# The second MLP product by Strassen's seven products of halves, with activations and sums kept in DRAM

## The chip, the cores and the metric

One core of a Trainium2 chip runs the whole kernel in one launch. The metric is the device time of one execution, in microseconds (us). Engines are named as in the profile: PE (TensorE, matrix products; PEld is its weight load), DVE (VectorE), ACT (ScalarE), POOL (GpSimd, here an issuer of DMAs), SP (SyncE, the other issuer of DMAs).

## The reference

One layer over 1024 latent tokens and 256 context tokens, width 1024. A mixer with two head groups (RG-LRU and S5), an output projection, a first layer norm, and then the part that the change touches:

```
def sq_relu_mlp(x, w1, b1, w2, b2):
    return jnp.square(jax.nn.relu(x @ w1 + b1)) @ w2 + b2
...
        x = layer_norm(DEEPNORM_ALPHA * x + g1 * m_lat, ln1_g[l], ln1_b[l])
        f_lat = sq_relu_mlp(modulate(x, sh2, sc2), mlp_w1[l], mlp_b1[l], mlp_w2[l], mlp_b2[l])
        x = layer_norm(DEEPNORM_ALPHA * x + g2 * f_lat, ln2_g[l], ln2_b[l])
```

Here `x` is 1024 x 1024, `w1` 1024 x 4096, `w2` 4096 x 1024, all float32.

## The kernel before

Everything is computed transposed: features lie on the 128 partitions, tokens on the free axis. Float32 products are made of three products of rounded parts: each operand is split into a high part (a cast to the format fp32r) and a low part (the value less its high part), and PE multiplies high by high, high by low and low by high, all into one PSUM sum. `split` makes such a pair for weights: ACT casts (`wh`), DVE subtracts (`wl`). `weights` loads 512 KB on SP's queue into `wr` (three buffers) and calls `split`.

The MLP starts when the first layer norm's results are there as `x2`: eight tiles, one for 128 features, with high and low parts of 1024 tokens. Tokens go in two halves j = 0, 1 of 512. The norm of half 0 is finished before the MLP; that of half 1 (its tiles are `yb`, `lt`, `lq`) runs on DVE and ACT under the first products of the MLP, as the generator `steps`.

The first product has 32 tiles of 128 hidden features. For one tile and one half, `prod` (L666 on, matmul at L675) makes 24 matmuls of 512 columns (8 tiles of `x2` by 3 parts). ACT then takes the relu (`r`) and the square (`hh`, the high part), DVE squares again in float32 and subtracts (`hl`, the low part).

The second product (`mlp2`, matmul at L1062) runs in nine blocks, `BLK = (3, 3, 3, 3, 4, 4, 4, 4, 4)`, right after the hidden tiles of its block. For each of 8 tiles of output features and each half it sums the block's tiles in PSUM, and DVE adds that to `acc` in SBUF. The last block goes in 256 columns and ends in the second layer norm (`centre`, `scale`) and the output DMAs. So hidden tiles never leave SBUF, and the hidden tiles and the weights of a block are all that is needed at once.

A scheduler sets the order of instructions on every engine from the order of the code and from when it takes things to be ready; each engine then runs its list strictly in order, so an instruction that waits holds everything behind it on its engine. A tile with `bufs=n` has n buffers; the writer of the next one waits for the last user of the oldest, a DMA that reads it among them. DMAs are issued in order on SP's queue (`ld`), on ACT's (`st_`), and on POOL's (`G.dma_start`), and `program` gives the descriptors of POOL's queue a small room in SBUF: `dynamic_dma_scratch_size=1024`, bytes a partition.

Of the kernel before, what the change touches and what calls it, by code (L numbers as in the profile page):

```python
# [41 lines left out]
def build(nc, tc, a, out):  # L42
# [967 lines left out]
    acc = {}  # L1010

    relu = [None]

    def mlp1(ids):
        ws = [weights(a["w1"][i]) for i in ids]
        hs = [[mp.tile([P, NL], F32R, tag=t, name=t, bufs=5) for t in ("hh", "hl")] for i in ids]
        yield hs
        for j in range(2):
            js = HS[j]
            for i, w, (hh, hl) in zip(ids, ws, hs):  # L1020
                ps = psm_.tile([P, 512], F32, tag="m1", name="ps_m1", bufs=3)
                prod(ps, w, x2, js)
                r = mp.tile([P, 512], F32, tag="r", name="r", bufs=2)
                S.activation(r, ps, AF.Relu, bias=col("b1", i))  # L1024
                relu[0] = S.activation(hh[:, js], r, AF.Square)  # L1025
# [4 lines left out]
    def weights2(i, last=False):  # L1030
        p, n = (mp, 3) if i % 4 < 3 else (mp2[0], 1)
        raw = wp.tile([P, 1024], F32, tag="wr", name="wr", bufs=3)
        ld(raw, a["w2"][i])
        hi = p.tile([P, D], F32R, tag="w2h", name="w2h", bufs=n)
        lo = p.tile([P, D], F32R, tag="w2l", name="w2l", bufs=n)
        if last:

            wm = mp2[0].tile([P, row(1)], F32, tag="wm", name="wm", bufs=4)[:, 0:1]
            stt(raw, raw, 1.0, g2r[0], MUL, MUL, accum_out=wm)
            ts(wm, wm, -1.0 / D, MUL)  # L1040
            S.activation(hi, raw, AF.Identity, bias=wm)
            stt(lo, raw, wm, f(hi), ADD, SUB)
        else:
            S.copy(hi, raw)  # L1044
            tt(lo, raw, f(hi), SUB)
# [4 lines left out]
    NB = len(BLK)  # L1050

    def mlp2(b, o, n, ws, hs, bk):
        last = b == NB - 1
        js = slice(o, o + n)
        for m in range(8):
            ps = psm_.tile([P, n], F32, tag="m2", name="ps_m2", bufs=3)
            c = 0
            for i in range(bk):
                hh, hl = hs[i]
                wh, wl = ws[i]  # L1060
                for x, w in ((hh, wh), (hl, wh), (hh, wl)):
                    PE.matmul(ps, w[:, m * P:(m + 1) * P], x[:, js], start=(c == 0), stop=(c == 3 * bk - 1))  # L1062
                    c += 1
            if b == 0:
                if m % 2 == 0:
                    acc[m // 2, o // 512] = (mp2[0] if o else mp).tile([P, 2, 512], F32, name=f"acc{m // 2}_{o // 512}")
            ac = acc[m // 2, o // 512][:, m % 2, o % 512:o % 512 + n]
            if b == 0:
                (S.copy if m % 2 else V.tensor_copy)(ac, ps)
            elif not last:  # L1070
                tt(ac, ps, ac, ADD)
            else:
                tt(ac, ps, ac, ADD)
            if b == NB - 2:
                nt = mp.tile([P, 512], F32, tag="r", name="nin", bufs=2)
                ld(nt, nscr[m, o // 512])
                ts(nt, nt, cr[:, m:m + 1], MUL, cd[:, m:m + 1], ADD)
                stt(ac, ac, g2c[:, m:m + 1], nt, MUL, ADD)
                if m == 0:
                    now = centre(n)  # L1080
                    next(now)
                now.send(ac)
            if last:
                if m == 0:
                    now = scale(mp2[0], n, "f", done2(js), o == NL - n)
                    next(now)
                now.send(ac)
            next(steps2[0], None)
            next(steps2[0], None)
        for _ in steps2[0]:  # L1090
            pass
        if b >= NB - 2:
            steps2[0] = now
        if last and o == NL - n:
            for _ in now:
                pass
# [12 lines left out]
    mp2 = []  # L1109
    i0 = 0  # L1110
    for b, bk in enumerate(BLK):
        ids = list(range(i0, i0 + bk))
        i0 += bk
        if b == 0:

            one = mlp1(ids)
            hs = next(one)
        else:
            hs = []
            for i in ids:  # L1120
                one = mlp1([i])
                hs += next(one)
                for _ in one:
                    pass
        if b:
            ws = [weights2(i, b == NB - 1) for i in ids]
        for o in range(0, NL, 256 if b == NB - 1 else 512):
            if b == 0:
                next(one)
                if o == 0:  # L1130
                    ws = [weights2(i) for i in ids]
            mlp2(b, o, 256 if b == NB - 1 else 512, ws, hs, bk)
            if b == 0 and o == 0:
                fence[0] = relu[0]
                for _ in steps:
                    pass
                dst_.close()
                mp2.append(pool("mp2", stack=mlp))
                g2r.append(mp2[0].tile([P, D], F32, name="g2r"))
                d = dr.tile([8, P], F32, name="g2d")  # L1140
                ld(d.rearrange("m p -> p m"), g2c)
                ld(g2r[0], d.rearrange("m p -> (m p)").partition_broadcast(P))
# [90 lines left out]
```

## Time and profile before

| what | us |
|---|---|
| median of 3 runs | 1647.38 (1646.48 to 1650.17) |
| the profiled execution | 1642.92 |
| its span, first to last instruction | 1641.1 |
| PE's first product of the MLP starts at | 908.68 |
| first half-1 product of the MLP starts at | 947.22 |

Times in the rows are counted from the span's start. A matmul of 512 columns is shown with 0.39 us, but the next one starts 0.23 us after it: matmuls are pipelined, so their cost is read from the distance of their starts, or from the chain of waits, where a run of xN of them has one length. "Busy" of PE is therefore high wherever matmuls follow one another.

### The profile page before, as it was taken

The numbers are of one execution on the slowest core, as the hardware profiler recorded it, in microseconds if no ns is written. First come the engines' busy times: TensorE is split into PE (matmuls) and PEld (weight loads), VectorE is DVE, ScalarE is ACT, GpSimd is POOL, SyncE is SP. The second block draws the span as 40 slices with busy tenths as digits, with TensorE's granted clock in tenths as the row PEclk, the third lists the DMA queues.
The fourth block names the chain that finished last, engine by engine and source line by source line (L and its number), as shares of the span: only waits on it lengthen the run. The fifth ranks groups of instructions, "written<-read, shape, count | busy, mean of one in ns | idle before, by whom it ended". The sixth has DMA issues, their size and how long they took to land.

```text
span 1641.1 us, 20069 instructions
## 1 busy us (share of the span) xinstructions
PE 1552.9 (95%) x7508; PEld 1268.1 (77%) x7508; DVE 1109.4 (68%) x2371; ACT 710.2 (43%) x978; POOL 8.7 (1%) x37
## 2 busy tenths in 40 slices
PE   7899998999879999799999899999999999999997
PEld 2687777777758787697788678888888888888887
DVE  7999999998939899329878844333432334247856
ACT  5576666666792426743335642113130303031225
POOL 0000000000000000000000000000000000000000
PEclk9999999999999999899999999999999999999999
DMA  7533323333745836855686421111110202022202
GB/s 270 203 119 112 106 109 117 120 115 108 271 139 176 239 129 165 220 155 200 197 281 192 169 92 63 39 39 64 52 52 20 70 13 90 13 77 84 71 1 103
DMA packets 92721, 199.27 MB, mean 121 GB/s; under 512 B 12496, under 2 KB 43728, under 8 KB 91472
## 3 DMA queue, kind: packets, MB, share of 16 engines
q1 hardware_dynamic: 77424, 176.10, 33.4%
q10 hardware_dynamic: 14048, 17.70, 3.0%
q0 software_dynamic: 1152, 4.19, 1.1%
q8 instruction: 59, 0.97, 0.2%
q14 instruction: 38, 0.31, 0.1%
HBM read 153.98 MB, written 43.98 MB: 121 GB/s over the span
## 4 chain that ended last, share of the span: by engine, by line
PE 58%; DVE 24%; ACT 7%; DMA 6%; issue 5%; SPq 0%; ACTq 0%; DVEq 0%
PE ps_m L675 22%; PE ps_m L1062 21%; PE ps_g L435 3%; PE ps_mm L380 3%; DVE sT L47 2%; DMA mo<-in_ada_t 2%; DVE wl L47 2%; DVE H L47 2%; DVE xc L56 2%; DVE sU L47 2%; DVE ii L47 2%; ACT H L603 1%; PE ps_gl L694 1%; DVE rr L56 1%; DVE ii L455 1%
## 5 line engine op out<-in xcount | busy, mean ns | idle before, releaser
L675 PE MATMUL ps_m<-x,wh 128*128 128x512 f32 x1024 | 323.2, 396 | 5.5 <-DVE yb L47 5.5
L675 PEld LDWEIGHTS ps_m<-x,wh 128*128 128x128 f32 x1024 | 192.6, 188 | 54.1 <-issue 6.1
L1062 PE MATMUL ps_m<-hh,w2h 128*128 128x512 f32 (+1 forms) x576 | 211.2, 367 | 0.0
L1062 PE MATMUL ps_m<-hl,w2h 128*128 128x512 f32 (+1 forms) x576 | 210.9, 366 | 0.0
L1062 PE MATMUL ps_m<-hh,w2l 128*128 128x512 f32 (+1 forms) x576 | 210.9, 366 | 0.0
L675 PE MATMUL ps_m<-x,wl 128*128 128x512 f32 x512 | 203.0, 397 | 0.0
L47 DVE TENSOR_TENSOR acc<-ps_m,acc 128x512 f32<-128x512 f32 (+1 forms) x144 | 90.7, 630 | 141.6 <-PE ps_m L1062 140.8
L98 ACT CAST wh<-wr 128x1024 fp32r<-128x1024 f32 x88 | 92.1, 1050 | 208.3 <-PE ps_m L675 102.7
L47 DVE TENSOR_TENSOR wl<-wr,wh 128x1024 fp32r<-128x1024 f32 x88 | 107.2, 1220 | 107.0 <-ACT wh L98 106.8
L380 PE MATMUL ps_mm<-x0h,wh 128*128 128x512 f32 x352 | 139.8, 397 | 1.0 <-ACT wh L98 1.0
L380 PE MATMUL ps_mm<-x0h,wl 128*128 128x512 f32 x352 | 139.5, 397 | 0.9 <-DVE wl L47 0.9
L380 PE MATMUL ps_mm<-x0l,wh 128*128 128x512 f32 x352 | 139.5, 396 | 0.0
L1044 ACT CAST w2h<-wr 128x1024 fp32r<-128x1024 f32 x28 | 28.7, 1049 | 236.1 <-PE ps_m L1062 206.5
L1062 PEld LDWEIGHTS ps_m<-hh,w2h 128*128 128x128 f32 x576 | 108.6, 189 | 18.3 <-ACT hh L1025 0.6
L1062 PEld LDWEIGHTS ps_m<-hl,w2h 128*128 128x128 f32 x576 | 108.6, 189 | 18.0 <-issue 0.5
L1062 PEld LDWEIGHTS ps_m<-hh,w2l 128*128 128x128 f32 x576 | 108.6, 189 | 17.7 <-issue 0.2
L675 PEld LDWEIGHTS ps_m<-x,wl 128*128 128x128 f32 x512 | 96.3, 188 | 24.0 <-issue 0.2
L47 DVE TENSOR_TENSOR r<-r 128x512 f32<-128x512 f32 x64 | 44.3, 691 | 84.0 <-ACT hh L1025 83.0
L1024 ACT ACTIVATE r<-ps_m,cols 128x512 f32<-128x512 f32 x64 | 43.8, 684 | 98.9 <-PE ps_m L675 91.5
L675 PE MATMUL ps_wo<-ms,wh 128*128 128x512 f32 x256 | 81.0, 397 | 2.6 <-ACT ms L799 2.6
L380 PEld LDWEIGHTS ps_mm<-x0h,wl 128*128 128x128 f32 x352 | 66.7, 189 | 14.2 <-DVE wl L47 1.4
L380 PEld LDWEIGHTS ps_mm<-x0h,wh 128*128 128x128 f32 x352 | 66.8, 190 | 13.4 <-ACT wh L98 1.4
(293 smaller groups left out, 2984.2 us busy)
## 6 DMA issues: line engine op xcount, KB each, us to landing
wr<-in_w SPq DMA_DIRECT2D x64, 512.0 KB, 3.5
mo<-in_ada_t SPq DMA_DIRECT2D x32, 512.0 KB, 4.2
wr<-in_w_in SPq DMA_DIRECT2D x24, 512.0 KB, 4.3
wr<-in_w_out SPq DMA_DIRECT2D x24, 512.0 KB, 4.6
xt<-xt ACTq DMA_DIRECT2D x16, 512.0 KB, 2.7
yd<-Y SPq DMA_DIRECT2D x16, 512.0 KB, 2.6
xt<-xt SPq DMA_DIRECT2D x16, 512.0 KB, 5.1
yf<-yd SPq DMA_DIRECT2D x8, 1024.0 KB, 9.5
```

The costliest lines, as they stand in the source:

```text
L47: (eng or V).tensor_tensor(out=o, in0=x, in1=y, op=op)
L56: V.scalar_tensor_tensor(out=o, in0=x, scalar=s, in1=y, op0=op0, op1=op1, **kw)
L98: S.copy(hi, raw)
L380: PE.matmul(ps, w[:, ks], x, start=(k == 0 and c == 0), stop=(k == KT - 1 and c == 2))
L435: PE.matmul(ps, w[:, w0:w0 + P], x[:, src:src + n], start=(c == 0), stop=(c == 2))
L455: V.tensor_tensor_scan(out=i, data0=q, data1=i, initial=0.0, op0=MUL, op1=ADD)
L603: S.copy(hv[0:64], ps[0:64])
L675: PE.matmul(ps, u[:, ks], v[:, js], start=(c == 0), stop=(c == 3 * KT - 1))
L694: PE.matmul(ps, u[:, ks], v[:, HS[j]], start=(i == 0 and c == 0), stop=(i == KT - 1 and c == 2))
L1024: S.activation(r, ps, AF.Relu, bias=col("b1", i))
L1044: S.copy(hi, raw)
L1062: PE.matmul(ps, w[:, m * P:(m + 1) * P], x[:, js], start=(c == 0), stop=(c == 3 * bk - 1))
```

## The change

The 32 hidden tiles are treated as 14 pairs (28 tiles) and 4 that stay as before. For the 28, the second product is one of matrices of halves: even and odd hidden tile of each pair, low and high half of the output features, and the two token halves. That would be eight products of halves; the form with seven products (Strassen's, in Winograd's order) takes four sums of the activations and four of the weights.

- Hidden tiles: per pair p, ACT writes the squares in plain float32 into a tile `hq` with seven slots (three buffers) and into `h12`; DVE makes four sums of 128x512 (`pair_sums`); POOL's queue stores all seven slots, 1.8 MB, to DRAM (`hscr`). The low parts are not made here any more.
- Weights: per pair, SP's queue loads the two tiles of `w2` (`w2r`, four buffers), DVE makes four sums of 128x512 (`weight_sums`, tile `ss`, two buffers), POOL's queue stores 1 MB to DRAM (`sscr`).
- The first product of pairs 0 to 2 (`NPRE = 3`) runs for half 0 of all six tiles first, then for half 1, where before three tiles of half 0 and the first block of `mlp2` stood; their weights are loaded and split twice.
- Then come the 4 plain hidden tiles, then seven products, each of 7 units. A unit loads 512 KB of weights or weight sums and 512 KB of activations or their sums, splits both (`wh`, `wl`, `bh`, `bl`), and is 24 matmuls of 512 columns into four PSUM banks. Two units are asked for ahead. DVE joins the products' results into `acc`; after products 2, 4, 5 and 3 the four finished tiles get the residual (`finish`).
- The last 4 tiles go as before, in 256 columns.

```
+    def pair_sums(p):
+        h, x = hq.pop(p), h12.pop(p)
+        tt(h[:, 3], x, h[:, 0], SUB)
+        tt(h[:, 5], h[:, 2], x, SUB)
+        tt(h[:, 4], h[:, 2], h[:, 3], SUB)
+        tt(h[:, 6], h[:, 1], h[:, 4], SUB)
+        G.dma_start(out=hscr[p // 2].rearrange("i p k c -> p i k c")[:, :, p % 2], in_=h)
...
+    def weight_sums(n):
+        for _ in range(n):
...
+            e, o = (pa.tile([P, 1024], F32, tag="w2r", name="w2r", bufs=4) for _ in range(2))
+            ld(e, a["w2"][2 * p])
+            ld(o, a["w2"][2 * p + 1])
+            ss = pa.tile([P, 4, 512], F32, tag="ss", name="ss", bufs=2)
+            lo, hi = HS
+            tt(ss[:, 0], e[:, hi], o[:, hi], ADD)
+            tt(ss[:, 1], ss[:, 0], e[:, lo], SUB)
+            tt(ss[:, 2], e[:, lo], e[:, hi], SUB)
+            tt(ss[:, 3], o[:, lo], ss[:, 1], SUB)
+            G.dma_start(out=sscr[p // 2].rearrange("i p k c -> p i k c")[:, :, p % 2], in_=ss)
+
+    for p in range(NPRE):
+        for e in range(2):
+            hidden(2 * p + e, w1_next(), 0, pair_half(p, e, 0))
+    fence[0] = relu[0]
+    for _ in steps:
+        pass
+    dst_.close()
+    for p in range(NPAIR):
+        for e in range(2):
+            w = w1_next()
+            for j in range(1 if p < NPRE else 0, 2):
+                hidden(2 * p + e, w, j, pair_half(p, e, j))
+        pair_sums(p)
+        if p >= NPRE:
+            weight_sums(2 if p < 2 * NPRE else 1)
...
+    PRODUCTS = (("1", ("w", 0, 0), 0), ("2", ("w", 1, 0), 1), ("6", ("s", 1), 4), ("7", ("s", 2), 5), ("4", ("w", 1, 1), 6),
+                ("5", ("s", 0), 3), ("3", ("s", 3), 2))
+    NQ = NPAIR // 2
...
+    def product(n):
+        pss = [bank(512, "ps_m2") for _ in range(4)]
+        for q in range(NQ):
+            (wh, wl), (xh_, xl_) = unit_next()
+            for k in range(2):
+                for m in range(4):
+                    for c, (w, x) in enumerate(((wh, xh_), (wh, xl_), (wl, xh_))):
+                        PE.matmul(pss[m], w[:, 512 * k + P * m:512 * k + P * m + P], x[:, 512 * k:512 * k + 512],
+                                  start=(q == 0 and k == 0 and c == 0), stop=(q == NQ - 1 and k == 1 and c == 2))
...
-    BLK = (3, 3, 3, 3, 4, 4, 4, 4, 4)
...
-                for x, w in ((hh, wh), (hl, wh), (hh, wl)):
-                    PE.matmul(ps, w[:, m * P:(m + 1) * P], x[:, js], start=(c == 0), stop=(c == 3 * bk - 1))
...
```

Three places in the lists of the engines. The first is DVE's list at the start of the MLP, between the norm's sums of squares (`lt`) of half 1 and its variance (`lv`, from `ps_var`). Before (`r`, `hl`: second square and low part of a hidden tile; `w2l`: low part of weights):

```order
L47 TENSOR_TENSOR lt_8547<-lt_8547,lq_8559 128x512
L47 TENSOR_TENSOR r_8659<-r_8659 128x512
L47 TENSOR_TENSOR w2l_8727<-wr_8724,w2h_8726 128x1024
L47 TENSOR_TENSOR lt_8547<-lt_8547,lq_8563 128x512
L47 TENSOR_TENSOR hl_8629<-r_8659,hh_8628 128x512
L47 TENSOR_TENSOR r_8689<-r_8689 128x512
L47 TENSOR_TENSOR lt_8547<-lt_8547,lq_8567 128x512
L47 TENSOR_TENSOR hl_8631<-r_8689,hh_8630 128x512
```

Behind it, in the changed kernel, the same place on DVE (`ss`: weight sums, from the raw weights `w2r`):

```order
L47 TENSOR_TENSOR lt_8547<-lt_8547,lq_8559 128x512
L47 TENSOR_TENSOR wl_8740<-wr_8737,wh_8739 128x1024
L47 TENSOR_TENSOR lt_8547<-lt_8547,lq_8563 128x512
L47 TENSOR_TENSOR ss_9254<-w2r_9250,w2r_9251 128x512
L47 TENSOR_TENSOR ss_9254<-w2r_9250 128x512
L47 TENSOR_TENSOR lt_8547<-lt_8547,lq_8567 128x512
L47 TENSOR_TENSOR ss_9254<-ss_9254,w2r_9250 128x512
L47 TENSOR_TENSOR ss_9264<-w2r_9260,w2r_9261 128x512
L47 TENSOR_TENSOR lt_8547<-lt_8547,lq_8571 128x512
L47 TENSOR_TENSOR wl_8774<-wr_8771,wh_8773 128x1024
```

The scheduler has moved weight sums that the code asks for only after the fourth pair up into the norm of half 1. Between the last `x2` of half 0 and the last `x2` of half 1, 26 of them and six weight splits stand in DVE's list, where before three squares, three low parts, three weight splits and four copies of `acc` stood. The second place is POOL's list behind the rows of the mixer. Before, it ends with two stores of 512 KB:

```order
L683 DMA pt6_5284<-pt_5281 128x1024
L683 DMA pt7_5289<-pt_5286 128x1024
```

In the changed kernel 28 stores follow on POOL's list, here the first 14 of them (`ss`: weight sums, 128 x 4 pieces of 2 KB; `hq`: a pair's seven slots, 128 x 7 pieces):

```order
L1083 DMA ws0_8620<-ss_9254 128x4x512
L1083 DMA ws0_8620<-ss_9264 128x4x512
L1083 DMA ws1_8621<-ss_9405 128x4x512
L1083 DMA ws1_8621<-ss_9415 128x4x512
L1083 DMA ws2_8622<-ss_9556 128x4x512
L1083 DMA ws2_8622<-ss_9566 128x4x512
L1083 DMA ws3_8623<-ss_9707 128x4x512
L1064 DMA hq0_8613<-hq_8639 128x7x512
L1083 DMA ws3_8623<-ss_9848 128x4x512
L1064 DMA hq0_8613<-hq_8708 128x7x512
L1083 DMA ws4_8624<-ss_9989 128x4x512
L1064 DMA hq1_8614<-hq_8777 128x7x512
L1083 DMA ws4_8624<-ss_10130 128x4x512
L1083 DMA ws5_8625<-ss_10271 128x4x512
```

Each store of `ss` frees one of two buffers, so the sums of the next but one wait for it, and with them all that is behind them on DVE. The third place is again DVE's list in the changed kernel, around the split `wl_9337` of the weights of the first hidden tile of pair 5:

```order
L47 TENSOR_TENSOR hq_9125<-h12_9154,hq_9125 128x512
L47 TENSOR_TENSOR ss_10412<-w2r_10408,w2r_10409 128x512
L47 TENSOR_TENSOR ss_10412<-w2r_10408 128x512
L47 TENSOR_TENSOR ss_10412<-ss_10412,w2r_10408 128x512
L47 TENSOR_TENSOR ss_10412<-w2r_10409,ss_10412 128x512
L47 TENSOR_TENSOR ss_10553<-w2r_10549,w2r_10550 128x512
L47 TENSOR_TENSOR ss_10553<-w2r_10549 128x512
L47 TENSOR_TENSOR ss_10553<-ss_10553,w2r_10549 128x512
L47 TENSOR_TENSOR ss_10553<-w2r_10550,ss_10553 128x512
L47 TENSOR_TENSOR wl_9337<-wr_9334,wh_9336 128x1024
```

`ss_10553` takes the buffer of `ss_10271`, whose store is the last of the 14 rows above, and `wl_9337` stands behind it.

## Rows read from the trace of the kernel before

**Rows 1.** Page, part 1: busy time, share of span, instructions by engine
```profile
PE 1552.9 (95%) x7508; PEld 1268.1 (77%) x7508; DVE 1109.4 (68%) x2371; ACT 710.2 (43%) x978; POOL 8.7 (1%) x37
```
**Rows 2.** Windows: stretch, length, busy and count of PE, PEld, DVE, ACT, POOL; clock; DMA
```profile
955.00:1580.00 625.00, 625.00 (x2719) 508.05 (x2718) 267.90 (x360) 139.47 (x184) 0.00 (x0) 1.00 0.17 53
913.80:954.30 40.50, 40.50 (x182) 32.40 (x181) 31.45 (x55) 24.54 (x38) 0.00 (x0) 1.00 0.35 123
```
**Rows 3.** Chain of waits in order of time: start, length, what, how many
```profile
947.22 16.97 PE ps_m L675 x72
...
1356.26 44.80 PE ps_m L675 x192
1401.06 43.54 PE ps_m L1062 x192
```
**Rows 4.** Page, part 5: one of three groups of the second product's matmuls
```profile
L1062 PE MATMUL ps_m<-hh,w2h 128*128 128x512 f32 (+1 forms) x576 | 211.2, 367 | 0.0
```
**Rows 5.** Timeline of PE: matmuls on G and on ms; start, length
```profile
702.10 0.63 PE L694 MATMUL ps_gl<-G,wh 128*128 128x512 f32 x2
...
702.80 0.63 PE L694 MATMUL ps_gl<-G,wh 128*128 128x512 f32 x2
...
900.96 0.62 PE L675 MATMUL ps_wo<-ms,wh 128*128 128x512 f32 x2
...
901.64 0.62 PE L675 MATMUL ps_wo<-ms,wh 128*128 128x512 f32 x2
```
**Rows 6.** Timeline of PE: the first products of the MLP, after a wait
```profile
908.68 1.19 PE L675 MATMUL ps_m<-x,wh 128*128 128x512 f32 x2 [5.52 <-DVE yb L47]
...
910.10 1.05 PE L675 MATMUL ps_m<-x,wh 128*128 128x512 f32 x2
...
911.38 1.05 PE L675 MATMUL ps_m<-x,wh 128*128 128x512 f32 x2
```
**Rows 7.** Timeline of DVE from the last x2 of half 0 to that of half 1
```profile
913.06 0.75 DVE L56 SCALAR_TENSOR_TENSOR x<-ya,c,xc 128x512 fp32r<-128x512 f32 x1
...
921.95 0.69 DVE L47 TENSOR_TENSOR lt<-lt,lq 128x512 f32<-128x512 f32 x1
...
937.20 3.66 DVE L47 TENSOR_TENSOR yb<-yb,ps_rs 128x512 f32<-128x512 f32 x6
...
953.55 0.75 DVE L56 SCALAR_TENSOR_TENSOR x<-yb,c,xc 128x512 fp32r<-128x512 f32 x1 [0.79 <-ACT xc L106]
```
**Rows 8.** Groups of DVE and ACT after 905 us: busy, mean ns, idle before
```profile
L47 DVE TENSOR_TENSOR acc<-ps_m,acc 128x512 f32<-128x512 f32 x112 | 77.2, 689 | 137.2 <-PE ps_m L1062 136.8
L47 DVE TENSOR_TENSOR wl<-wr,wh 128x1024 fp32r<-128x1024 f32 x32 | 39.2, 1225 | 91.4 <-ACT wh L98 91.3
L98 ACT CAST wh<-wr 128x1024 fp32r<-128x1024 f32 x32 | 33.5, 1046 | 105.6 <-PE ps_m L675 102.7 <-DMA wr<-in_w 2.9
```
**Rows 9.** Timeline of POOL: three of its DMA issues
```profile
419.34 0.67 POOL L462 DMA_DIRECT2D hs<-ii  x1 [120.04 <-ACT H L603]
...
559.91 1.80 POOL L665 DMA_DIRECT2D mh<-mx  x2 [13.58 <-ACT mh L664]
659.96 0.56 POOL L683 DMA_DIRECT2D pt<-pt  x1 [98.25 <-ACT pt L681]
```
**Rows 10.** DMA issues: queue, count, KB each, median us from issue to landing
```profile
wr<-in_w SPq DMA_DIRECT2D x64, 512.0 KB, 3.5
...
pt<-pt ACTq DMA_DIRECT2D x6, 512.0 KB, 2.7
...
pt<-pt POOLq DMA_DIRECT2D x2, 512.0 KB, 9.0
...
hs<-ii POOLq DMA_DIRECT2D x1, 512.0 KB, 5.2
```
**Rows 11.** Page, part 3: queues of SP and POOL: packets, MB, share of 16 engines' span
```profile
q1 hardware_dynamic: 77424, 176.10, 33.4%
...
q0 software_dynamic: 1152, 4.19, 1.1%
```

More of the change, by code (lines that the diff above doesn't have):

```diff
@@ L842, in build @@
     hst.close()
-    x2p = pool("x2", side="right", stack=es)
+    x2st = ExitStack()
+    x2p = pool("x2", side="right", stack=x2st)
     x2 = [x2p.tile([P, 2, NL], F32R, name=f"x2_{k}") for k in range(KT)]
@@ L1009, in build, with bank @@
     psm_ = pool("psm", space=PSUM, stack=mlp)
[L1010 to L1017, printed above, removed]
+    NB1 = FF // P
+    NPAIR = 14
+    NPRE = 3
+    bank_n, relu, fence_r = [0], [None], [None]
+    def bank(n, name):
+        t = "abc"[bank_n[0] % 3]
+        bank_n[0] += 1
+        return psm_.tile([P, n], F32, tag="m" + t, name=name, bufs=2)
@@ new lines, in hidden, with w1_next @@
+    def hidden(i, w, j, done_):
+        ps = bank(512, "ps_m1")
+        prod(ps, w, x2, HS[j])
+        r = mp.tile([P, 512], F32, tag="r", name="r", bufs=3)
+        S.activation(r, ps, AF.Relu, bias=col("b1", i))
+        done_(r)
+    hist = ExitStack()
+    order = [i for i in range(2 * NPRE)] + [i for i in range(NB1)]
+    ahead, w_n = [], [0]
+    def w1_next():
+        while len(ahead) < 2 and w_n[0] < len(order):
+            ahead.append(weights(a["w1"][order[w_n[0]]]))
+            w_n[0] += 1
+        return ahead.pop(0)
@@ new lines, in build, with pair_half, done_ @@
+    pa = pool("pa", stack=hist)
+    hscr = [dr.tile([7, P, 2, 512], F32, name=f"hq{q}") for q in range(NPAIR // 2)]
+    sscr = [dr.tile([4, P, 2, 512], F32, name=f"ws{q}") for q in range(NPAIR // 2)]
+    hq, h12 = {}, {}
+    def pair_half(p, e, j):
+        if p not in hq:
+            hq[p] = pa.tile([P, 7, 512], F32, tag="hq", name="hq", bufs=3)
+        if (e, j) == (0, 1):
+            h12[p] = pa.tile([P, 512], F32, tag="h12", name="h12", bufs=2)
+        dst = {(0, 0): hq[p][:, 0], (1, 0): hq[p][:, 1], (1, 1): hq[p][:, 2], (0, 1): h12.get(p)}[e, j]
+        def done_(r):
+            relu[0] = S.activation(dst, r, AF.Square)
+        return done_
@@ L1018, in mlp1, with done_ @@
+    hs = []
+    for i in range(2 * NPAIR, NB1):
+        hh, hl = (hp2.tile([P, NL], F32R, name=f"{t}{i}") for t in ("hh", "hl"))
+        hs.append((hh, hl))
+        w = w1_next()
         for j in range(2):
             js = HS[j]
[L1020 to L1025, printed above, removed]
+            def done_(r):
+                S.activation(hh[:, js], r, AF.Square)
@@ L1026, in mlp1 @@
                 tt(r, r, r, MUL)
                 tt(hl[:, js], r, f(hh)[:, js], SUB)
-            yield
-    def weights2(i, last=False):
-        p, n = (mp, 3) if i % 4 < 3 else (mp2[0], 1)
+            hidden(i, w, j, done_)
+    x2st.close()
+    cp_ = pool("cp", side="right", stack=mlp)
+    acc = {(m, j): cp_.tile([P, 2, 512], F32, name=f"acc{m}_{j}") for j in range(2) for m in range(4)}
+    us = [cp_.tile([P, 512], F32, name=f"u2_{m}") for m in range(4)]
+    vs = [cp_.tile([P, 512], F32, name=f"u3_{m}") for m in range(4)]
@@ new lines, in build, with acc_of, finish @@
+    g2r = cp_.tile([P, D], F32, name="g2r")
+    d = dr.tile([8, P], F32, name="g2d")
+    ld(d.rearrange("m p -> p m"), g2c)
+    ld(g2r, d.rearrange("m p -> (m p)").partition_broadcast(P))
+    steps2 = [iter(())]
+    centres = {}
+    def acc_of(m, j):
+        return acc[m // 2, j][:, m % 2]
+    def finish(m, j):
+        ac = acc_of(m, j)
+        nt = mp.tile([P, 512], F32, tag="r", name="nin", bufs=3)
+        ld(nt, nscr[m, j])
+        ts(nt, nt, cr[:, m:m + 1], MUL, cd[:, m:m + 1], ADD)
+        stt(ac, ac, g2c[:, m:m + 1], nt, MUL, ADD)
+        if j not in centres:
+            centres[j] = centre(512)
+            next(centres[j])
+        centres[j].send(ac)
@@ new lines, in product @@
+    def product(n):
[7 more added lines that the diff above has]
+                                  start=(q == 0 and k == 0 and c == 0), stop=(q == NQ - 1 and k == 1 and c == 2))
+            next(steps2[0], None)
+            next(steps2[0], None)
+        for m, ps in enumerate(pss):
+            if n == "1":
+                (S.copy if m % 2 else V.tensor_copy)(us[m], ps)
+            elif n == "2":
+                tt(acc_of(m, 0), ps, us[m], ADD)
+            elif n == "6":
+                tt(us[m], ps, us[m], ADD)
+            elif n == "7":
+                tt(vs[m], ps, us[m], ADD)
+            elif n == "4":
+                tt(acc_of(4 + m, 0), ps, vs[m], ADD)
+            elif n == "5":
+                tt(acc_of(4 + m, 1), ps, vs[m], ADD)
+                tt(us[m], ps, us[m], ADD)
+            elif n == "3":
+                tt(acc_of(m, 1), ps, us[m], ADD)
+        for _ in steps2[0]:
+            pass
+        if n in "2453":
+            m0, j = {"2": (0, 0), "4": (4, 0), "5": (4, 1), "3": (0, 1)}[n]
+            for m in range(m0, m0 + 4):
+                finish(m, j)
+            if n in "43":
+                steps2[0] = centres[j]
@@ L1032, in weights2 @@
+    def weights2(i):
         raw = wp.tile([P, 1024], F32, tag="wr", name="wr", bufs=3)
         ld(raw, a["w2"][i])
[L1034 to L1045, printed above, removed]
@@ L1046, in weights2 @@
-        return hi, lo
-    BLK = (3, 3, 3, 3, 4, 4, 4, 4, 4)
[L1050 to L1060, printed above, removed]
-                for x, w in ((hh, wh), (hl, wh), (hh, wl)):
-                    PE.matmul(ps, w[:, m * P:(m + 1) * P], x[:, js], start=(c == 0), stop=(c == 3 * bk - 1))
[L1063 to L1096, printed above, removed]
@@ L1098, in build @@
-    steps2, g2r = [iter(())], []
+        hi, lo = (cp_.tile([P, D], F32R, tag=t, name=t, bufs=NB1 - 2 * NPAIR) for t in ("w2h", "w2l"))
+        wm = cp_.tile([P, row(1)], F32, tag="wm", name="wm", bufs=4)[:, 0:1]
+        stt(raw, raw, 1.0, g2r, MUL, MUL, accum_out=wm)
+        ts(wm, wm, -1.0 / D, MUL)
+        S.activation(hi, raw, AF.Identity, bias=wm)
+        stt(lo, raw, wm, f(hi), ADD, SUB)
+        return hi, lo
     def done2(js):
@@ L1107, in done2 @@
         return done
[L1109 to L1142, printed above, removed]
+    for n, _, _ in PRODUCTS:
+        if n == "3":
+            ws = [weights2(i) for i in range(2 * NPAIR, NB1)]
+        product(n)
+    for o in range(0, NL, 256):
+        js = slice(o, o + 256)
+        for m in range(8):
+            ps = bank(256, "ps_m2")
+            c = 0
+            for (hh, hl), (wh, wl) in zip(hs, ws):
+                for x, w in ((hh, wh), (hl, wh), (hh, wl)):
+                    PE.matmul(ps, w[:, m * P:(m + 1) * P], x[:, js], start=(c == 0), stop=(c == 3 * len(hs) - 1))
+                    c += 1
+            ac = acc_of(m, o // 512)[:, o % 512:o % 512 + 256]
+            tt(ac, ps, ac, ADD)
+            if m == 0:
+                now = scale(cp_, 256, "f", done2(js), o == NL - 256)
+                next(now)
+            now.send(ac)
+            next(steps2[0], None)
+            next(steps2[0], None)
+        for _ in steps2[0]:
+            pass
+        steps2[0] = now
+    for _ in now:
+        pass
+    bst.close()
     mlp.close()
```

31 lines of the change are left out of this document (30 added, 1 removed).

## The prediction

> **What bounds the kernel now.** I read the busy shares first: PE 95%, DVE 68% [rows 1]. The windows then show the MLP for itself: from 955 to 1580 us PE is busy 625.00 of 625.00 us at a granted clock of 1.00, DVE 267.90 and ACT 139.47 [rows 2]. So in that stretch only matmuls count, and DVE's or ACT's work is worth nothing as long as it keeps up. The price of a matmul comes from the chain of waits, not from the length of one: 192 of the first product in 44.80 us, 0.2333 each, and 192 of the second in 43.54 us, 0.2268 each [rows 3]. The one place where PE had to wait is the start of the MLP: 5.52 us before its first product [rows 6], after which it met the norm of half 1 on DVE with no slack. The first half-1 product starts at 947.22 [rows 3], and its operands are still being made then: the last `x2` starts at 953.55 on DVE [rows 7].
>
> All sums are made against the profiled execution: span 1641.1, time 1642.92, so 1.8 us lie around the span and stay. The median of the runs is 1647.38, 4.5 above; I add the change to the median.
>
> **What the change takes away.** The second product has 576 matmuls in each of three groups [rows 4]: 1344 of 512 columns and 384 of 256. After it, seven products of 7 units of 24 are 1176 of 512 columns, and the 384 stay. 168 fewer at 0.2268 are **-38.1 us**. The first product keeps its 1536 of 512 columns. What DVE and ACT no longer do for 28 hidden tiles and 112 sums into `acc` (0.689 each [rows 8]) saves nothing, since PE does not wait for it there [rows 2].
>
> **The pitch of the new operands.** Two pitches of the same 512-column matmul occur in the kernel: in threes, on `G` 0.70 us (702.10 to 702.80), on `ms` 0.68 (900.96 to 901.64) [rows 5], as the 0.2333 on `x2` and 0.2268 on `hh` [rows 3]. The moving tiles lie at different places in SBUF: `x2` and `G` above 131 KB of a partition, `hh` and `ms` below 103 KB. The new `bh` and `bl` lie between, from 97 to 129 KB. No row has an operand there, so 1176 matmuls cost between 0 and 1176 × 0.0065 = 7.7 us more; I take 0.231, 5.1 us, nearer the upper end since most of the room lies beyond 103 KB. Net: **-33.0 us**.
>
> **The units of the products.** One unit is 24 × 0.231 = 5.5 us of PE. Beside it stand two casts on ACT, 2 × 1.05, two subtractions on DVE, 2 × 1.22 [rows 8], and two loads on SP's queue, 1 MB per 5.5 us or 190 GB/s; one such load takes 3.5 us [rows 10], and in the busiest stretch read 123 GB/s ran beside full PE [rows 2]. All of that hides, with two units asked ahead; if it did not, each of 49 units would be late by what is over 5.5 us. At the seven ends of products DVE also takes 4 to 8 sums of 0.69 and, four times, 4 × (0.69 + 0.75 + 0.69) = 8.5 us of `finish`, sized by [rows 7, 8], against 11 us of two units: between 0 and 12 us in all, taken as 2.
>
> **The start of the MLP.** DVE is busy 31.45 of 40.50 us from 913.8 to 954.3 [rows 2]. From there ten operations of 0.61 (3.66 for six [rows 7]) and three of 1.22 [rows 8] go, 9.8 us; 26 weight sums at 0.61 and six splits at 1.22 come, 23.2. That makes 44.9 us of work in a stretch of 40.5, so the last `x2` is at least 4.4 us later; if the idle time (9.0 us, mostly waits of 0.79 for ACT between `x2`s [rows 7]) stays, 13.4. PE wants that `x2` as early as before: its six half-0 products take 33.6 us plus 5.3 (slow first products and the norm's small matmuls; before, 144 large ones stood in the same 908.68 to 947.22 us). I take 12 us late, since the 0.79s belong to a chain through ACT that remains.
>
> **The stores.** This is what decides. The sums of the next but one pair wait until a store of `ss` has landed, and behind them in DVE's list stand the splits of the first product's weights. `wl_9337` (pair 5) stands behind `ss_10553`, which waits for the 14th store on POOL's queue: 11 of 1.05 MB and 3 of 1.84 MB. PE, undisturbed, wants it after 480 matmuls on `x2`: 908.7 + 480 × 0.2333 + 5.3 = 1026. The first store can start when its sums are made: 921.95 [rows 7] + nine operations of 0.61 + three splits of 1.22 = 931. That leaves 95 us for 14 stores.
>
> What one takes has no row. The nearest: POOL stores of 512 KB to DRAM landed after 5.2 and 9.0 us [rows 10]. Of the 5.2, 0.67 are issue [rows 9]; the data take 1.6 to 2.3 at the rate that a queue moves bytes when its packets run (q0: 4.19 MB in 1.1% of 1641.1 us; q1: 176.10 MB in 33.4% [rows 11]); 2.3 to 2.9 remain. With four times the pieces and twice the bytes an `ss` store has 0.67 (issue fixed) to 2.68 us of issue, 3.3 to 4.5 of data and the rest: 6.3 to 10.1 us, taken as 8.0, about the middle. An `hq` store with seven: 0.67 to 4.69, 5.7 to 7.9 and the rest, 8.7 to 15.5, taken as 11.8. Whether one runs beside the next is not shown either. At most two stores of one row's piece were issued back to back (`mh`, 559.91 [rows 9]), in a room for descriptors of 1024 bytes a partition; these have four and seven times the pieces, so I take them one after another. Lower end: they overlap, and the chain is no longer than DVE's own work.
>
> One after another: 11 × 8.0 + 3 × 11.8 = 123.4, plus 4 × 0.61 = 2.4 where the last sums of a store stand behind sums that themselves wait (`ss_9405` and `ss_9556`), plus four sums and the split, 3.7: 931 + 129.5 = 1060.5, against 1026. PE waits **34.5 us** by then, the 12 of the `x2`s within it. SP's loads of `w2r` wait with the sums, since the buffers come free with them, and loads of `w1` behind; that is the same chain. After that the stores no longer fall behind: the other 3 `ss` and 11 `hq` are 154 us, and the 8 pairs left are 8 × 96 × 0.2333 = 179 us of PE, with four plain tiles behind them before a product reads the last `hq`. After a wait PE starts slow: its first products took 1.28 us for three, 0.427 each, at 910.10 [rows 6], for about 12 of them, 2.4 us.
>
> The Trainium skill, "DMA: Bandwidth & Descriptors", section "Anatomy of one DMA — SWDGE (gpsimd) path", has such a store at about 2 us plus the bytes at 436 GB/s; by that an `ss` store is an estimated 4.4 us, an `hq` one 6.2, the chain 67, and PE would hardly be reached by it, which is the first rival's time. For 512 KB it gives 3.2 us, and the rows show 5.2 and 9.0 [rows 10], so the trace speaks against it. The same page, sections "SWDGE vs HWDGE vs iDMA" and "The descriptor swizzle", has descriptors of 16 bytes in rings in SBUF, and 8 data descriptors and one completion per engine for 128 rows; so 1024 bytes would be an estimated 64 descriptors, an `ss` store 33 and an `hq` store 57: no two fit. No run here shows that.
>
> **Forecast (A).** -33.0 + 34.5 + 2.4 + 2.0 = +5.9: 1647.4 + 5.9 = **1653 us**. With the pitch at its ends (-5.1, +2.6), one step of 0.5 us on each store (7 each way) and the ends of products, 1641 to 1671.
>
> **Rivals.** B, faster: the stores overlap, or one after another they take under 1026 + 12 - 931 - 6.1 = 101 us together (6.5 and 9.7 each). The chain then ends before PE arrives, itself 12 us late from the `x2`s. What is left is 12 + 2.4 + 2.0: -16.6, **1631**. For it: two `mh` stores went out within 1.80 us [rows 9], and 5.2 us for 512 KB [rows 10] leaves room. Against: the 9.0.
>
> C, slower: the stores at their upper ends, 10.1 and 15.5, one after another: 157.6 us and a wait of 68.7; -33.0 + 68.7 + 4.4 = +40, **1687**. For it: the 9.0 us at 512 KB, and loads of 190 GB/s and the stores use the same 16 engines. Against: a DMA share of 0.35 at the busiest [rows 2].
>
> D: neither `x2`s nor stores are late and the operands run at 0.2268: -38, **1609**. Against: 44.9 us of work do not fit in 40.5.
>
> That the change does not do what it says is excluded by PE's list, which has the 168 matmuls fewer; the one open thing there is time.
>
> **Chances.** A 0.50, B 0.32, C 0.15, D 0.03: the serial issue rests on no row, and within it 8.0 lies between 6.3 and 10.1, so B and C together have about as much as A. The range goes from B's less its pitch (1625) through A to the lower part of C (1675, stores at 9.4 and 13.9). About 0.2% (3.3 us) is what a measurement of this kernel can tell from no change, so 1644 to 1651 is "same": A gives it 0.12 and faster 0.07, slower 0.31; B and D are faster, C slower. Sum, rounded: faster 0.42, same 0.13, slower 0.45. A alone: 1641 to 1671.
>
> **What would show it.** POOL's stores: the time from issue to landing (8.0 and 11.8 by A), and whether a second is in flight beside the first. DVE: idle before `ss` sums, ended by a DMA; under B only for `x2`. PE: a wait of some 12 us before the first half-1 product, and one, or several, before the first products of pairs 3 to 5, 34 us in all; then 0.231 a matmul in seven products without gaps and a tail as before. Wrong would be a wait inside the products (loads or `finish` not hidden), waits at the first product beyond pair 5, or a pitch above 0.2333.

## The result, and the profile after

The changed kernel takes 1631.97 us (median of 4 runs, 1630.04 to 1632.74), against 1648.78 for the kernel before (4 runs, 1646.48 to 1651.94): a ratio of 0.9895, 95% interval 0.9875 to 0.9915. It is faster by some 17 us. The forecast was 1653, slower; the time lies in its range, 1625 to 1675, and the sign was wrong.

The profiled execution has a span of 1628.3 us. The gain lies behind PE's first product of the MLP. From there to the end of the span the kernel before takes 1641.1 - 908.68 = 732.4 us [rows 6], the changed one 1628.3 - 911.94 = 716.4: 16.0 less. The 168 matmuls that are gone are worth 38.1, so 22.1 us were lost on the way. This length, from the first product to the end, is used for all kernels below, since what comes before it is the same work and moves by a few us: the first product starts between 908.68 and 915.93 us in the ten traces. Each length is that of one profiled execution, and the first 12 products of the MLP alone took from 2.9 to 5.3 us in them: 5.2 in the kernel before and in the changed one, where PE had just waited 5.52 and 5.74 us and the granted clock from 907 to 917 us was 0.66 (for a part of it at the lower of its two levels, 1.2 GHz), and 2.9 in one kernel below, where it had waited 2.97 and the clock was 1.00 (2.4 GHz). Differences of 1 or 2 us are therefore not read.

Page of the changed kernel, part 1 (as [rows 1]):

```profile
PE 1521.5 (93%) x7340; PEld 1240.5 (76%) x7340; DVE 1127.6 (69%) x2357; ACT 783.0 (48%) x1048; POOL 32.7 (2%) x65
```

Windows of the changed kernel (stretch, length, busy and count of PE, PEld, DVE, ACT, POOL; clock; DMA share and GB/s, as [rows 2]):

```profile
945.00:980.00 35.00, 23.17 (x75) 17.25 (x73) 18.76 (x28) 15.83 (x22) 2.65 (x4) 0.76 0.90 332
980.00:1050.00 70.00, 67.86 (x290) 53.77 (x288) 34.93 (x50) 26.54 (x37) 8.26 (x10) 1.00 0.85 319
1100.00:1290.00 190.00, 190.00 (x816) 153.10 (x815) 52.10 (x61) 64.81 (x89) 7.49 (x8) 1.00 0.40 146
1290.00:1500.00 210.00, 210.00 (x926) 173.32 (x925) 115.08 (x120) 78.75 (x81) 0.00 (x0) 1.00 0.60 194
```

The first of these stretches in the kernel before:

```profile
945.00:980.00 35.00, 35.00 (x152) 27.86 (x151) 16.85 (x21) 16.00 (x23) 0.00 (x0) 1.00 0.24 79
```

PE is full from 1100 to 1500 us, in the first products and in the seven products alike. It is not from 945 to 980: 23.17 of 35 us, with 75 matmuls where the kernel before has 152, and at a granted clock of 0.76. The loss is there. The chain of waits says through what (start, length, what, how many):

```profile
955.34 0.75 POOL ws L1083
956.09 5.07 issue
961.18 0.76 POOL ws L1083
961.94 10.75 issue
972.71 0.75 POOL ws L1083
973.46 7.19 issue
980.66 4.83 DMA ws<-ss
985.54 0.57 issue
986.12 1.23 DVE wl L47
987.39 33.41 PE ps_m L675 x142
...
1042.11 4.86 DMA ws<-ss
1047.00 1.91 DVE ss L47 x3
1048.99 0.54 issue
1049.54 1.23 DVE wl L47
1050.81 9.36 PE ps_m L675 x39
...
1297.00 201.32 PE ps_m L1179 x888
...
1541.54 26.32 PE ps_m L1179 x116
```

It runs through the stores of weight sums on POOL into DVE's list and from there, through a split `wl`, to PE, at 987 and again at 1050 us. Behind that PE is its own bound to the tail. What PE waited for itself (timeline, idle time and its end in brackets):

```profile
953.64 0.97 PE L675 MATMUL ps_m<-x,wh 128*128 128x512 f32 x3 [2.86 <-ACT x L105]
958.59 0.79 PE L675 MATMUL ps_m<-x,wh 128*128 128x512 f32 x1 [3.98 <-DVE x L56]
973.02 0.79 PE L675 MATMUL ps_m<-x,wh 128*128 128x512 f32 x1 [4.99 <-DVE x L56]
987.39 0.50 PE L675 MATMUL ps_m<-x,wl 128*128 128x512 f32 x1 [1.40 <-DVE wl L47]
...
1050.81 0.50 PE L675 MATMUL ps_m<-x,wl 128*128 128x512 f32 x1 [1.55 <-DVE wl L47]
```

Together 14.8 us; of the other 7.3, some 5.7 are slow matmuls between the waits: the 75 from 945 to 980 took 23.17 us, at 0.2333 each they would have taken 17.5. The first wait is for ACT and the next two for `x2` on DVE. In DVE's list these `x2` stand behind weight sums that wait for stores (four rows of the list, the last one the last `x2`):

```profile
953.63 0.69 DVE L47 TENSOR_TENSOR ss<-w2r 128x512 f32<-128x512 f32 x1 [4.11 <-DMA ws<-ss]
...
971.01 0.69 DVE L47 TENSOR_TENSOR ss<-w2r 128x512 f32<-128x512 f32 x1 [5.03 <-DMA ws<-ss]
...
972.22 0.74 DVE L56 SCALAR_TENSOR_TENSOR x<-yb,c,xc 128x512 fp32r<-128x512 f32 x1
...
981.59 0.74 DVE L56 SCALAR_TENSOR_TENSOR x<-yb,c,xc 128x512 fp32r<-128x512 f32 x1
```

The last `x2` comes 69.7 us after PE's first product; in the kernel before it came 44.9 us after. The wait at 1050.81, for pair 5, is the place on which the prediction rested; by then most of it had been taken earlier, at `x2`.

### The profile page after: what moved, and what is told of

It reads as the page before. It is cut to its first block, busy times and chain, and to the rows that moved or that the text cites. A ratio compares the mean times of both kernels' runs of the same rounds, so it can differ in the third digit from the quotient of the medians.

```text
span 1628.3 us, 20161 instructions
## 1 busy us (share of the span) xinstructions
PE 1521.5 (93%) x7340; PEld 1240.5 (76%) x7340; DVE 1127.6 (69%) x2357; ACT 783.0 (48%) x1048; POOL 32.7 (2%) x65
## 4 chain that ended last, share of the span: by engine, by line
PE 50%; DVE 25%; DMA 8%; ACT 8%; issue 8%; POOL 0%; SPq 0%; ACTq 0%; DVEq 0%; POOLq 0%
PE ps_m L675 19%; PE ps_m L1179 14%; PE ps_g L435 3%; PE ps_mm L380 3%; DMA mo<-in_ada_t 3%; DVE sT L47 2%; DVE wl L47 2%; DVE H L47 2%; DVE xc L56 2%; PE ps_m L1242 2%; DVE sU L47 2%; DVE ii L47 2%; ACT H L603 2%; PE ps_gl L694 1%; DVE rr L56 1%
## 5 line engine op out<-in xcount | busy, mean ns | idle before, releaser
L47 DVE TENSOR_TENSOR wl<-wr,wh 128x1024 fp32r<-128x1024 f32 x143 | 174.6, 1222 | 272.0 <-ACT wh L98 271.9
L98 ACT CAST wh<-wr 128x1024 fp32r<-128x1024 f32 x143 | 149.9, 1050 | 378.5 <-PE ps_m L1179 133.9
L1179 PE MATMUL ps_m<-bh,wh 128*128 128x512 f32 x392 | 152.7, 391 | 0.4 <-DVE u L47 0.2
L1179 PE MATMUL ps_m<-bl,wh 128*128 128x512 f32 x392 | 152.5, 389 | 0.0
L1179 PE MATMUL ps_m<-bh,wl 128*128 128x512 f32 x392 | 152.2, 389 | 0.2 <-DVE wl L47 0.2
L675 PEld LDWEIGHTS ps_m<-x,wl 128*128 128x128 f32 x512 | 98.0, 191 | 27.5 <-DVE wl L47 3.8
L1179 PEld LDWEIGHTS ps_m<-bh,wh 128*128 128x128 f32 x392 | 73.6, 188 | 16.8 <-DVE u L47 1.2
L1179 PEld LDWEIGHTS ps_m<-bh,wl 128*128 128x128 f32 x392 | 73.5, 188 | 15.7 <-DVE wl L47 0.4
L1179 PEld LDWEIGHTS ps_m<-bl,wh 128*128 128x128 f32 x392 | 73.6, 188 | 15.2 <-issue 0.2
L380 PEld LDWEIGHTS ps_mm<-x0l,wh 128*128 128x128 f32 x352 | 67.2, 191 | 12.6
L47 DVE TENSOR_TENSOR sT<-al,H 128x128 f32<-128x128 f32 x254 | 66.7, 284 | 1.3
L675 PE MATMUL ps_gl<-G,wh 128*128 128x512 f32 x192 | 60.5, 396 | 0.1
```

The lines of the kernel that those rows point to most:

```text
L380: PE.matmul(ps, w[:, ks], x, start=(k == 0 and c == 0), stop=(k == KT - 1 and c == 2))
L1179: PE.matmul(pss[m], w[:, 512 * k + P * m:512 * k + P * m + P], x[:, 512 * k:512 * k + 512], start=(q == 0 and k == 0 and c == 0), stop=(q ...
```

## The experiments

Two theories to begin with. **Theory 1**: the stores go one at a time on POOL's queue, hold DVE's list through the two buffers of `ss`, and so delay the last `x2` and the splits. **Theory 2**: DVE's added work alone does it. The table gathers what was measured; "lost" is the length from PE's first product less 732.4 - 38.1 = 694.3.

| kernel | time, us | ratio to before | first product to end | lost |
|---|---|---|---|---|
| changed | 1631.97 | 0.9895 (0.9875 to 0.9915) | 716.4 | 22.1 |
| sums not stored | 1615.29 | 0.9808 (0.9789 to 0.9828) | 701.7 | 7.4 |
| sums later | 1616.54 | 0.9825 (0.9807 to 0.9843) | 701.8 | 7.5 |
| stores in pieces | 1629.15 | 0.9892 (0.9875 to 0.9908) | 714.1 | 19.8 |
| `x2` earlier on ACT | 1625.38 | 0.9864 (0.9830 to 0.9897) | 709.3 | 15.0 |
| sums not stored, `x2` earlier | 1611.00 | 0.9783 (0.9747 to 0.9818) | 697.6 | 3.3 |
| sums later, `x2` earlier | 1607.78 | 0.9767 (0.9742 to 0.9792) | 693.2 | -1.1 |
| the same, one pair at a time | 1610.05 | 0.9777 (0.9754 to 0.9801) | 693.8 | -0.5 |

**Sums not stored.**

```
-            G.dma_start(out=sscr[p // 2]...[:, :, p % 2], in_=ss)
...
-                ld(rv, sscr[q][u[1]])
+                ld(rv, a["w2"][4 * q:4 * q + 4:2, :, HS[0]]...)
```

> The weight sums are made on DVE as in the changed kernel, but not stored; the four products that would read them read plain weights of the same size, so their values are wrong and their work is the same. Theory 1 (the stores, one at a time on POOL's queue, hold DVE's list through the two buffers, and with it the last x2 and the weight splits of the first product: 21.5 us of the MLP): what stays is the work of DVE alone in the norm of half 1, 5 to 10 us by the list (29 sums and 6 splits there); the MLP from PE's first product to the end goes from 716.4 to 700-706 us, the whole to about 1617. Theory 2 (DVE's added work itself makes x2 late, the stores cost little): no change within 3 us, 1632.

Measured: 701.7 us from the first product, lost 7.4 instead of 22.1. Theory 1 holds for the larger part: 14.7 us are the stores'. The order of DVE's list is nearly the same (29 sums ahead of the last `x2` instead of 26), so theory 2 is left with 7.4 at most. The run takes the bytes of these stores away too, so it can't tell their going one at a time from their traffic; the stores in pieces, below, bear on that.

**Sums later.**

```
+        last = V.tensor_tensor(out=h[:, 6], in0=h[:, 1], in1=h[:, 4], op=SUB)   # last of pair_sums
...
+            with after(last):
+                weight_sums(2 if p < 2 * NPRE else 1)
```

> The weight sums of DVE are ordered behind the last sum of the activations of the same pair, so none stands in the norm of half 1; stores, buffers and all other work are those of the changed kernel. Theory 1: neither x2 nor a split waits for a store in the first ten half-products; PE's wait of 14.8 us behind the start and its slow products go; the MLP takes 716.4 - 21.5 + 0 to 3 = 695 to 698 us, the whole about 1611. Theory 3 (the wait only moves: POOL's queue then has 17 stores beside pairs 3 to 5, the splits of pairs 4 to 7 stand behind the sums and wait there): 705 to 716 us in the MLP, with PE waits between 1050 and 1130 us.

Measured: 701.8, lost 7.5: neither of the two figures. No sum stands in the norm now, and yet the last `x2` comes late. From 940 to 966 us the largest of DVE's waits is for ACT (what waited for what: us, times, longest; in the kernel before it was 4.0 us in five waits):

```profile
DVE x L56 <- ACT xc L106: 9.0, 8, 2.0
```

ACT makes the high part of `x2` (L105) first. Here is ACT's list in the changed kernel, and the one before:

```profile
952.25 0.63 ACT L1055 ACTIVATE hq<-r 128x512 f32<-128x512 f32 x1
952.79 1.51 ACT L105 ACTIVATE x<-yb,c 128x512 fp32r<-128x512 f32 x2
```

```profile
929.69 0.63 ACT L1025 ACTIVATE hh<-r 128x512 fp32r<-128x512 f32 x1
...
937.92 1.52 ACT L105 ACTIVATE x<-yb,c 128x512 fp32r<-128x512 f32 x2 [1.87 <-DVE yb L47]
```

Before, the high parts wait for DVE's `yb`. In the changed kernel they follow the square of the sixth half-0 tile at once: a line of the diff, `fence[0] = relu[0]`, orders them behind the last square that was asked for, and the change asks for six tiles of half 0 where three stood. The sixth square can only come when PE has run out of half-0 work, so PE must wait: the 2.86 us that end with "ACT x L105". That is **theory F**, and no step of the prediction had it.

**The order on ACT alone.**

```
             hidden(2 * p + e, w1_next(), 0, pair_half(p, e, 0))
-    fence[0] = relu[0]
+            if (p, e) == (1, 0):
+                fence[0] = relu[0]
```

> The changed kernel, but the high parts of x2 of half 1 on ACT are ordered behind the square of the third half-0 tile, as before the change, and no longer behind that of the sixth. Theory F (that order alone makes x2 late by some 6.5 us, which is what stays of the lag when no weight sum stands in the norm) and theory 1 (the stores hold DVE's list there for longer than that) together: the x2s still wait for stores, so little changes, the lag of 21.9 us falls by 0 to 5, the whole 1627 to 1632. If F were most of the loss: 1625 or less.

Measured: lost 15.0, 7.1 less; more than the 0 to 5 that I gave it. With `x2` earlier, the last `x2` comes 52.0 us after the first product instead of 69.7, and a wait comes out at the place that the prediction named. PE before the first hidden tile of pair 5, and DVE ahead of it:

```profile
1043.55 0.80 PE L675 MATMUL ps_m<-x,wl 128*128 128x512 f32 x1 [5.47 <-DVE wl L47]
```

```profile
1039.74 1.29 DVE L47 TENSOR_TENSOR ss<-w2r 128x512 f32<-128x512 f32 x2 [2.59 <-DMA ws<-ss]
1040.95 0.68 DVE L47 TENSOR_TENSOR ss<-ss,w2r 128x512 f32<-128x512 f32 x1
1041.67 0.69 DVE L47 TENSOR_TENSOR ss<-w2r,ss 128x512 f32<-128x512 f32 x1
1042.28 1.22 DVE L47 TENSOR_TENSOR wl<-wr,wh 128x1024 fp32r<-128x1024 f32 x1
```

A store lands, four sums, the split, and PE goes on 5.47 us late. But the edit moved more than `x2`: in this kernel 48 weight sums and the landing of the 13th store stand ahead of that split, in the changed one 52 and that of the 14th. That one store is 5.2 us of the changed kernel's chain (the 13th landed at 1041.80, the 14th at 1046.97). So the 7.1 us are not the price of the order on ACT alone; that is read below, where no sum stands in the norm.

**DVE's work alone.** Sums not stored, and the order on ACT as above:

> As the kernel without the stores of the weight sums (sums made, not stored, the products that would read them read plain weights of the same size), and with x2's high parts ordered behind the third tile's square. Prediction's term for DVE's work alone: 29 sums and 6 splits in the norm make the last x2 4.4 to 13.4 us later than in the kernel before, taken as 12: lag 12 over the kernel before, the MLP 694.3 + 12 = 706 us. Theory F (in the kernel without stores, the lag of 7.8 us came from the order behind the sixth square, and the sums fill DVE's idle time): lag 1 to 4, the MLP 695 to 698, the whole 1610.

Measured: lost 3.3. In this kernel 22 sums and 6 splits stand between the last `x2` of half 0 and that of half 1, and the last `x2` comes 49.8 us after PE's first product, 4.9 later than before. So DVE's work by itself costs PE 3.3, not 12.

**Both causes away.** Sums later and `x2` earlier, and the same with one pair's sums behind each pair's activations from the first pair on:

```
-        if p >= NPRE:
-            weight_sums(2 if p < 2 * NPRE else 1)
+        with after(last):
+            weight_sums(1)
```

> Weight sums ordered behind the activations' sums of their pair, and x2's high parts behind the third tile's square: both suspected causes taken away. Theory 1 + F: no PE wait between the first product and the tail, lag 0 to 1 us over the kernel before, the MLP 732.4 - 38.1 = 694 to 696 us, the whole about 1610 (the kernel without the first cause was 1616.5, lag 6.5). If something else keeps x2 late: 1615 to 1617.

> The same, with one pair's weight sums behind each pair's activations from the first pair on, instead of two behind pairs 3 to 5. POOL's queue then has one store of each kind for each 22.4 us of PE. Theory 1 + F: no more gain in time than the kernel with sums two at a time, 1608 to 1612, since the two-at-a-time sums make PE wait for nothing either. Rival: the loads and stores of the first pairs collide with the norm and the time is 1 to 4 us longer.

Measured: nothing is lost, 693.2 us, and 1607.78 in all, 2.3% less than the kernel before; by the length it is 23.1 us less than the changed kernel. The windows of this kernel over the stretch that had the loss:

```profile
945.00:980.00 35.00, 35.00 (x151) 27.90 (x150) 18.91 (x24) 21.67 (x32) 1.92 (x2) 1.00 0.54 192
980.00:1050.00 70.00, 70.00 (x302) 56.40 (x301) 26.19 (x36) 22.04 (x31) 5.12 (x6) 1.00 0.70 258
1050.00:1270.00 220.00, 220.00 (x945) 177.26 (x944) 85.15 (x111) 74.54 (x103) 17.13 (x20) 1.00 0.65 233
```

One pair at a time gives no more (693.8). That both are below 694.3, by 1.1 and 0.5, goes with their start and not with the change: their first 12 products took 2.9 and 4.4 us against 5.2 in the kernel before. The order on ACT by itself costs 7.5 us (what the sums-later kernel lost, and this one does not), sums and stores with `x2` earlier 15.0. Together that is 22.5 against 22.1, but the 15.0 belongs to a chain that is one store shorter, so the agreement does not show that the two add up in the changed kernel.

**Stores in pieces.** Is it the room for descriptors that makes the stores follow one another?

```
-            G.dma_start(out=sscr[p // 2]...[:, :, p % 2], in_=ss)
+            for i in range(4):
+                G.dma_start(out=sscr[p // 2][i][:, p % 2], in_=ss[:, i])
```

and the same with seven pieces for `hq`.

> Each store is cut into its slots: four DMAs of 128 x 512 for weight sums, seven for a pair's activations, all on POOL's queue as before; the same bytes, the same buffers. Theory R (a store of four or seven pieces fills the room for descriptors of POOL's queue, so the next one is issued only when it has landed): the small DMAs go out 0.6 to 0.9 us apart without waiting for the landing of the one before, a set of weight sums is free again 5 to 6 us after its last sum whatever is ahead, the 14th set lands about 20 us earlier, PE's lag of 21.5 us falls to 5 to 12; the whole 1617 to 1622. Theory L (the bytes or the share of the DMA engines, 0.9 in this stretch, set the time): the sets land as before, 1629 to 1635.

Measured: lost 19.8, 1629.15: theory L's time, with theory R's mechanism. Against the kernel before the ratio is 0.9892, for the changed kernel 0.9895, so no saving is shown. In the changed kernel all 28 stores have none other in flight, and where sums were ready the next is issued 0.3 us after the one before has landed (POOL's timeline; the store issued at 1042.11 landed at 1046.97, as the chain above shows):

```profile
1034.53 0.80 POOL L1083 DMA_DIRECT2D ws<-ss  x1 [7.00 <-issue]
1042.11 0.76 POOL L1083 DMA_DIRECT2D ws<-ss  x1 [6.78 <-issue]
1047.28 0.76 POOL L1083 DMA_DIRECT2D ws<-ss  x1 [4.41 <-issue]
```

With pieces several are issued back to back:

```profile
1001.94 0.54 POOL L1085 DMA_DIRECT2D ws<-ss  x1
1002.54 0.54 POOL L1065 DMA_DIRECT2D hq<-hq  x1
1003.14 1.14 POOL L1085 DMA_DIRECT2D ws<-ss  x2
1006.10 0.54 POOL L1085 DMA_DIRECT2D ws<-ss  x1 [1.81 <-DMA hq<-hq]
```

Counted over the landings of all 154 pieces, at most six others are in flight when one is issued, and the eighth waits until the oldest has landed. So POOL's queue, with this room, holds seven pieces of 128 rows and one store of 512 or 896. By the Trainium skill, "DMA: Bandwidth & Descriptors", sections "Terms" and "The descriptor swizzle", a descriptor has 16 bytes and a transfer over 128 partitions takes 9 of them per engine; 1024 bytes are then an estimated 64 descriptors, seven times 9 is 63, and the run agrees with that. The size of the room was not varied, so that it is the room that limits them is worked out and not shown.

Why nothing is saved, the next window suggests: the transfers now share DMA engines that are full. The window from 945 to 980 us of this kernel:

```profile
945.00:980.00 35.00, 23.22 (x81) 16.57 (x80) 22.27 (x35) 15.07 (x21) 10.27 (x19) 0.85 1.00 382
```

The DMA engines are busy throughout, 382 GB/s instead of 332, and DVE's sums wait 11.9 us for loads of `w2r` in this stretch, where the changed kernel has 1.8. That a store which is no longer held by the one before is now held by the bytes of all fits these rows; no run takes bytes alone away. The landing of a piece of weight sums has a median of 6.8 us, 256 KB, where a whole store of 1 MB took 5.8.

**The place of the moving operand.** The tiles `bh`, `bl` and `br` of the products (four buffers each) at 175 to 223 KB of a partition instead of 81 to 129; the accumulators take the lower place:

```
-    bp = pool("bp", stack=bst)
...
     x2st.close()
+    bp = pool("bp", side="right", stack=mlp)
     cp_ = pool("cp", side="right", stack=mlp)
```

> The activations of the seven products and their parts bh and bl lie at 175 to 223 KB of a partition, where x2 lay before, instead of 81 to 129 KB; the accumulators take the lower place. Theory P (the place of the moving operand sets the distance of two matmuls): 0.2333 us instead of 0.2267 in the seven products, 1176 x 0.0066 = +7.7 us. Rival (the distance on x2 and G has another cause): 0.2267 as in the changed kernel. Both: the first unit has to wait until the last matmul on x2 is done, for its load of 4.4 us, cast and subtraction, some 7 us once; so 1647 by P, 1639 by the rival, and the distance itself is read from the chain of waits.

Measured: 1644.71 us (8 runs), 0.9981 of before (0.9970 to 0.9993). 116 matmuls of the last product in a row, from the chain of this kernel:

```profile
1555.51 27.05 PE ps_m L1179 x116
```

27.05 / 116 = 0.2332 us, where the changed kernel's chain above has 26.32 / 116 = 0.2269 for the same ones. The place decides, as theory P has it. On 1176 matmuls that is 7.4 us. Most of the rest of the 12.7 that this kernel is slower than the changed one lies at the first unit: PE waits 3.1 us for it until 1301.10, and the first of the seven products then takes 42.5 us where the next four take 39.2 each.

## Why the prediction was wrong

Its sum was -33.0 + 34.5 + 2.4 + 2.0 = +5.9. By the runs it is -38.1 + 22.1 = -16.0.

- **The gain.** 38.1 was right: with both causes away the length is 693.2 against 732.4, 39.2 less. The pitch of `bh` and `bl` was not: I took 0.231 and 5.1 us, nearer the upper end, and 0.2267 was measured (201.32 / 888). The rule (place in SBUF) holds, but between 97 and 129 KB the tiles belong to the fast side. This is 5.1 us of the error. It was a term without a row, as the prediction said.
- **The stores.** This is the step that failed: the mechanism was right and its size was not. One after another, yes; the first was issued at 935.92 and the 14th landed at 1046.97, 111.1 us for a forecast 125.8, and PE was 22 us late, not 34.5. Of the 111.1 us, eleven stores of weight sums took 76.3, three of `hq` 27.5 and the gaps between them 7.3, for forecasts of 88, 35.4 and 2.4. That is 6.9 and 9.2 us a store, where 8.0 and 11.8 were taken: within the bounds of 6.3 to 10.1 and 8.7 to 15.5, near their lower ends. Over all 28 the medians, 5.8 and 6.9, are below them. Issue was not what made them long: it grew from 0.54 us for one piece to 0.76 and 0.94 for four and seven, not in proportion as the upper bounds had it; how the rest divides no run shows. The first store also went out 4.9 us later than the forecast 931, and PE started 3.3 us later. This step is 12.4 us of the error, and by itself it turns the sign, from +5.9 to -6.5. The path was another one in part: the sum has PE wait for the split of pair 5, but `x2` stands behind the same stores, and PE was late from there on.

```profile
hq<-hq POOLq DMA_DIRECT2D x14, 1792.0 KB, 6.9
...
ws<-ss POOLq DMA_DIRECT2D x14, 1024.0 KB, 5.8
```

- **The other price.** The fixed time of 2 us plus bytes, from the Trainium skill, "DMA: Bandwidth & Descriptors", section "Anatomy of one DMA — SWDGE (gpsimd) path", made an estimated 4.4 and 6.2 us of these; the medians of 5.8 and 6.9 lie above it, nearer to it than to mine, and the 6.9 and 9.2 of the 14 stores that decided lie between the two prices.
- **The start of the MLP.** DVE's work was taken as 12 us, bounds 4.4 to 13.4. Without stores the last `x2` was 4.9 us late, at the lower bound, and PE lost 3.3. What the step missed, and put at nothing, is the order on ACT, 7.5 us by itself. The view that would have shown it is ACT's list of the two kernels beside each other; I had read DVE's and POOL's only, since those carried the new work. In the changed kernel both lie within the wait for stores, whose chain ends at pair 5's split; what each of them adds there no run shows apart.
- **Clock and ends of products.** The 2.4 us of slow products after the wait are inside the 22.1, and the ends of products cost nothing: PE waits there for 0.2 us or less. 4.4 us of the error.
- **Rival B** had the measured time, 1631, by another way: a chain of stores that ends before PE arrives, a DVE term of 12 that was 3.3, and a pitch that was too slow. Of its two conditions, overlap did not occur; the other, stores one after another in under 101 us, was missed by little (76.3 + 27.5 = 103.8, and 111.1 with the gaps), but the chain did hold `x2` and the split. That its number came true is luck. So is that the time lies in the stated range: A alone, which had the mechanism, was 1641 to 1671. (Added up straight, its terms give 1639 to 1673.)
- **What would show it** named a wait of some 12 us before the first half-1 product, waits at pairs 3 to 5, DVE idle before `ss` ended by a DMA, products without gaps and a tail as before. The last three were there. PE's waits were 2.86 us before the first half-1 product and 8.97 for `x2` within the first two, one of 1.40 in the fourth, none at pairs 3 and 4, and 1.55 at pair 5: 14.8 in all, and 22 us lost, instead of 34.

## What to carry to other kernels

When a change adds background transfers, look up what stands behind each of their buffer waits in the list of the engine that fills the buffers: the sums were not needed before the third product, some 400 us later, and cost 15 us because they stood early in a list that PE depended on. Moving work later, to where it is asked for, gave back all of it; making the transfers overlap gave back nothing that is clear of noise. And when a change reorders a loop, re-read every ordering edge that refers to "the last one so far": here one such line, untouched in its text, cost 7.5 us once the sums stood later.
